# RWKV chunks of 64 tokens instead of 32, two heads on the partitions and four beside, 64x64 inverses joined from blocks of 32

## The chip, the cores and the metric

One core of a Trainium2 chip runs the whole program. The metric is the device time of one execution in microseconds; the median of several is compared. Five engines work side by side: TensorE (PE, with its weight loads PEld), VectorE (DVE), ScalarE (ACT), GpSimd (POOL) and SyncE (SP), which issues most transfers.

## The reference

A trunk of two mixing layers, each followed by a squared-ReLU MLP, on 512 tokens of width 1024 in float32. Layer 0 splits its input projection between a Griffin recurrence (512 columns wide) and RWKV-7 time mixing (8 heads of 64); layer 1 has gated DeltaNet and mLSTM. The change is in RWKV. After the token shift, decays and norms, what it computes is this recurrence over the tokens:

```
def step(S, inp):
    rt, wt, kt, vt, kkt, at = inp
    sk = jnp.einsum('bhvk,bhk->bhv', S, kkt)
    S = (S * wt[:, :, None, :] - sk[..., None] * (kkt * at)[:, :, None, :]
         + vt[..., None] * kt[:, :, None, :])
    return S, jnp.einsum('bhvk,bhk->bhv', S, rt)
```

y is then normed per head, gets a bonus (r, k, r_k) times v, is gated by g, joined with the Griffin output and projected back.

## The kernel before

Large matrices are split into a high and a low fp32r part and multiplied in three matmuls (wh h, wh l, wl h) of 128x128 by 512 columns. The projections are streamed: raw weights come by DMA, ScalarE or VectorE casts the high part (wh), VectorE or GpSimd makes the low part (wl). The names `hT` with `wh`, `wl` are the input projection; `wh`, `wl` with `yah`, `yal` the Griffin half of the output projection, with `ybh`, `ybl` its RWKV half, which comes last.

RWKV is computed in chunks of 32 tokens, 16 chunks, with products inside a chunk as matrices, so that a chunk's state change is a few small fp32 matmuls (an fp32 matmul shows as two MATMUL records and two weight loads). For two halves of the tokens (hf 0 and 1, eight chunks each) the steps are:

- `product_stream` (L882): alpha and rho (`va`) against kappa and beta (`kb`), 256 matmuls of 64x32 by 64 columns, masked on VectorE into `cm`, four heads one over the other on the partitions, two beside.
- `inverse_stream` (L962): the lower triangular 32x32 blocks go through memory into one block per lane (partition), `lanes` (L936) inverts them there with 62 dependent VectorE operations (`xtmp`, `xt` on `q`), and the inverses come back through memory as `xb`. `lanes` runs once per half.
- `turn_stream` (L905): `va` and `kb` transposed against the identity into `tm`, 512 matmuls.
- `ahead_stream` (L983): `wt`, `bv`, `u0` from `tm`, `cm` and `xb`, all that does not hang on the state.
- `scan_stream` (L1033): 16 steps; in each one group of 8 matmuls with the state `S`, an add on VectorE to `us`, groups with `us`, and an add on VectorE into the next `S`. The heads' norm and gate (`heads_stream`, L1090) hang behind.

Beside this runs Griffin: convolution (`xc`), gates (`r`, `i`, `th`), a scan on VectorE, and `gel` times the result split into `yah` and `yal`. All engines' instructions are issued through one helper (L73), so every row of the profile has line L73 and is told apart by its names.

The order of the instructions on each engine is decided while the kernel is built: `layer0` (L1255) spawns the streams, the one spawned first has the highest priority, and a planner keeps a clock per engine with the prices of `cost` (L173); a stream that needs a tile (`need`) or an event waits in the plan, and the lowest priority, the main stream with the large projections, fills the gaps. A psum bank is taken with `take` and returned with `give`; there are 8.

## Time and profile before

| | |
|---|---|
| time, median of 3 runs | 1405.82 us (1405.06 to 1406.92) |
| profiled execution | 1407.12 us, span 1405.3 us |
| TensorE busy | 1334.4 us (95% of the span) |
| VectorE busy | 768.4 us (55%) |
| ScalarE busy | 472.2 us (34%) |
| GpSimd busy | 184.2 us (13%) |
| mean granted TensorE clock | 0.975 |

TensorE is busy nearly always, but a busy stretch is not one of full use: many small matmuls, a lower granted clock and short stops lie in it. Layer 0 takes the stretch from the start to some 340 us, and RWKV's small matmuls lie between 95 and 310 us. An "issue" releaser is time in which an engine waited for nothing that the profile shows. The granted clock is a share of full speed.

### The profile page before, as it was taken

How to read it: one execution, taken by the hardware profiler on the slowest of the kernel's cores; microseconds unless marked ns; L12 is line 12 of the kernel's file. 1: busy time of each engine (PE TensorE's matmuls, PEld its weight loads, DVE VectorE, ACT ScalarE, POOL GpSimd, SP SyncE). 2: the span in 40 equal slices, each digit the busy share in tenths (PEclk: the TensorE clock that was granted, in tenths of full speed). 3: DMA queues.
4: the chain of work that ended last, by engine and by line, in shares of the span. 5: the costliest groups of instructions: out<-in, count | busy, mean ns of one | idle time of the engine just before them, and what ended most of it. 6: DMA issues, size and time to landing. Idle time of an engine off the chain costs nothing.

```text
span 1405.3 us, 23951 instructions
## 1 busy us (share of the span) xinstructions
PE 1334.4 (95%) x10036; PEld 1079.7 (77%) x10036; DVE 768.4 (55%) x1444; ACT 472.2 (34%) x818; POOL 184.2 (13%) x172
## 2 busy tenths in 40 slices
PE   6888999899999999999999999999789999999998
PEld 6666777668888888888896777878578888888886
DVE  5885956456434435344568748854744354453444
ACT  5522523324322323223453434431333232232222
POOL 2352221231000000000013412213300000000000
PEclk9999989999999999999999999999989999999999
DMA  6122200322233233232312231110322322322331
GB/s 228 61 82 86 69 19 24 100 87 76 88 96 99 90 93 102 90 91 98 112 54 83 76 97 61 49 57 16 120 76 63 102 90 90 105 91 90 97 99 60
DMA packets 58594, 118.35 MB, mean 84 GB/s; under 512 B 17398, under 2 KB 17654, under 8 KB 58486
## 3 DMA queue, kind: packets, MB, share of 16 engines
q1 hardware_dynamic: 57190, 114.71, 25.8%
q10 hardware_dynamic: 1296, 2.11, 0.5%
q8 instruction: 79, 1.29, 0.4%
q14 instruction: 29, 0.24, 0.1%
HBM read 113.13 MB, written 3.67 MB: 83 GB/s over the span
## 4 chain that ended last, share of the span: by engine, by line
PE 83%; DVE 7%; issue 3%; ACT 3%; DMA 3%; POOL 1%; SPq 0%; POOLq 0%; DVEq 0%
PE ps_a L73 61%; PE ps_g L73 23%; DMA q<-d1g 1%; DMA q<-d 1%; DVE xn L73 1%; DVE wl L73 1%; DVE x L73 1%; DVE ktok L73 1%; DMA gb<-in_g_norm_dram 0%; ACT junk L73 0%; DVE cv L73 0%; DVE gr L73 0%; DVE z L73 0%; ACT k L73 0%; ACT wh L73 0%
## 5 line engine op out<-in xcount | busy, mean ns | idle before, releaser
L73 DVE TENSOR_TENSOR wl<-raw,wh 128x512 fp32r<-128x512 f32 x325 | 232.0, 720 | 257.8 <-ACT wh L73 249.1
L73 PE MATMUL ps_a<-hT,wh 128*128 128x512 f32 (+1 forms) x1088 | 315.5, 375 | 0.0
L73 ACT CAST wh<-raw 128x512 fp32r<-128x512 f32 x283 | 172.4, 619 | 361.5 <-PE ps_a L73 317.9
L73 PEld LDWEIGHTS ps_a<-hT,wh 128*128 128x128 f32 x1088 | 197.3, 188 | 41.0
L73 PE MATMUL ps_g<-hT,wh 128*128 128x512 f32 x656 | 218.7, 413 | 7.7 <-DVE xt L73 3.7
L73 PE MATMUL ps_a<-hT,wl 128*128 128x512 f32 (+1 forms) x544 | 203.8, 375 | 0.0
L73 PEld LDWEIGHTS ps_g<-hT,wh 128*128 128x128 f32 x656 | 127.0, 195 | 43.2 <-issue 11.1
L73 PE MATMUL ps_a<-wh,acth 128*128 128x512 f32 x384 | 151.5, 395 | 0.0
L73 PE MATMUL ps_a<-wl,acth 128*128 128x512 f32 x384 | 151.5, 395 | 0.0
L73 PE MATMUL ps_a<-wh,actl 128*128 128x512 f32 x384 | 151.3, 394 | 0.0
L73 PE MATMUL ps_g<-hT,wl 128*128 128x512 f32 x328 | 134.8, 411 | 0.0
L73 POOL TENSOR_TENSOR wl<-raw,wh 128x512 fp32r<-128x512 f32 x43 | 57.6, 1346 | 580.9 <-ACT wh L73 557.3
L73 PEld LDWEIGHTS ps_a<-hT,wl 128*128 128x128 f32 x544 | 102.1, 188 | 20.4
L73 PEld LDWEIGHTS ps_a<-wh,actl 128*128 128x128 f32 x384 | 72.1, 188 | 17.1
L73 PEld LDWEIGHTS ps_a<-wh,acth 128*128 128x128 f32 x384 | 72.2, 188 | 16.8
L73 PEld LDWEIGHTS ps_a<-wl,acth 128*128 128x128 f32 x384 | 72.1, 188 | 16.8
L73 DVE CAST wh<-raw 128x512 fp32r<-128x512 f32 x85 | 37.1, 436 | 86.9 <-PE ps_a L73 82.0
L73 ACT ACTIVATE relu<-ps_a 128x512 f32<-128x512 f32 x60 | 35.9, 599 | 141.6 <-PE ps_a L73 141.6
L73 PEld LDWEIGHTS ps_g<-hT,wl 128*128 128x128 f32 x328 | 64.0, 195 | 17.4 <-issue 2.1
L73 PE MATMUL ps_g<-hT,w 128*128 128x256 f32 x384 | 51.2, 290 | 0.4 <-DVE hT L73 0.4
L73 PE MATMUL ps_g<-wh,acth 128*128 128x512 f32 x128 | 50.5, 395 | 0.0
L73 PE MATMUL ps_g<-wl,acth 128*128 128x512 f32 x128 | 50.5, 395 | 0.0
(395 smaller groups left out, 1820.4 us busy)
## 6 DMA issues: line engine op xcount, KB each, us to landing
...
```

The costliest lines, as they stand in the source:

```text
L73: return fn(*args, **kw)
```

## The change

The chunks are 64 tokens, 8 of them. Two heads lie on the partitions (64 rows each) and four beside each other, so all small tiles are 64x64 and `HEADS` names only the two diagonal quarters of the array. `product_stream` makes 128 matmuls with 128 columns, and splits each bank on VectorE in two masked operations, into `ab` (for m = 1; `bk` for m = 0) and `mm`; its last quarter waits for the first half's inverse. The lanes still invert 32x32 blocks, now the two diagonal blocks of each 64x64 one; the off-diagonal block (`A`, masked with `join`) is then brought in by three rounds of matmuls: `xb` transposed into `xs`, `A` times `xs` into `xg`, and `xg` times `xb`, added to `xb`. `ahead_stream` has one helper for wt, bv and u0, the scan has one bank and one addition per step, `v` is shifted by one VectorE operation, and the planner's price of a small matmul is higher. TensorE's small fp32 matmuls are 2024 before and 1184 after.

```diff
-        return self.sp.tile([P, 3, 4, 16, 32], dt, tag="wide", bufs=1, name=f"{name}{self.n}")
+        return self.sp.tile([P, 3, 4, 8, 64], dt, tag="wide", bufs=1, name=f"{name}{self.n}")
...
-            return max(n / 600, 0.107) + 0.002 if size(a) == P else 0.045
+            return max(n / 600, 0.107) + 0.002 if P in (size(a), a.shape[0]) else max(n / 1200, 0.053)
...
-        self.rmask = self.cst[:, 128:192]
-        o = 192
+        o = 128
         for name, n in (("inc64", P), ("suf64", P), ("inc128", P), ("suf128", P), ("ones", P), ("pair", 2), ("lt64", 64), ("le64", 64), ("join", 64)):
             setattr(self, name, self.cst[:, o:o + n])
+            if name == "lt64":
+                self.ltle = self.cst[:, o:o + P]
...
-        return ap.rearrange("p (c s) -> p c s", s=32)
+        return ap.rearrange("p (c s) -> p c s", s=64)
...
-            nc, c3 = self.nc, self.c3
-            v = self.va[:, 0, p]
-            nc.scalar.activation(out=v, in_=c3(ps), func=AF.Identity, scale=self.omu[:, 8 + p:9 + p])
-            mu = self.col("mu", 8 + p)
-            nc.vector.scalar_tensor_tensor(out=v[:, :, 1:32], in0=c3(ps)[:, :, 0:31], scalar=mu, in1=v[:, :, 1:32], op0=ALU.mult, op1=ALU.add)
-            nc.vector.scalar_tensor_tensor(out=v[:, 1:16, 0:1], in0=c3(ps)[:, 0:15, 31:32], scalar=mu, in1=v[:, 1:16, 0:1], op0=ALU.mult, op1=ALU.add)
+            self.shift_mix(ps, 8 + p, self.va[:, 0, p].rearrange("p c s -> p (c s)"))
...
-    HEADS = [(i, b, e, slice(64 * b, 64 * b + 64), slice(64 * i + 32 * b, 64 * i + 32 * b + 32), slice(64 * e, 64 * e + 64))
-             for e in range(2) for i in range(2) for b in range(2)]
+    HEADS = [(q, slice(64 * b, 64 * b + 64)) for q in range(4) for b in range(2)]
...
-        for hf in range(2):
-            for m in (1, 0):
-                for j in (2 * hf, 2 * hf + 1):
-                    ps = yield from self.take()
-                    v = ps.rearrange("p (c e t) -> p c e t", e=2, t=64)
-                    for c in range(4):
-                        for i, b, e, f, r, _ in self.HEADS:
-                            nc.tensor.matmul(v[r, c, e, :], lhsT=self.kb[f, m, 2 * i + e, 4 * j + c, :], rhs=self.va[f, 1:3, 2 * i + e, 4 * j + c, :],
-                                             start=True, stop=True)
-                        yield
-                    o = self.slot(shape=(P, 8, 64), name="cm")
-                    nc.vector.tensor_tensor(out=o, in0=ps.rearrange("p (c t) -> p c t", t=64), in1=self.rmask[:, None, :].broadcast_to([P, 8, 64]), op=ALU.mult)
-                    self.give(ps)
-                    self.cm[m][j] = o
-                self.set(f"cm{m}{hf}")
+        for m, hf in ((1, 0), (1, 1), (0, 0), (0, 1)):
+            if m == 0 and hf:
+                yield "xb0"
+            ab, mm = (self.bk, self.mv) if m == 0 else (self.ab, self.mu)
+            ab[hf] = self.slot(shape=(P, 4, 4, 64), tag="q", name="ab")
+            for j in (2 * hf, 2 * hf + 1):
+                mm[j] = self.slot(shape=(P, 2, 4, 64), name="mm")
+            for c in range(4 * hf, 4 * hf + 4):
+                ps = yield from self.take()
+                v = ps.rearrange("p (q t) -> p q t", q=4)
+                for q, r in self.HEADS:
+                    nc.tensor.matmul(v[r, q], lhsT=self.kb[r, m, q, c, :], rhs=self.va[r, 1:3, q, c, :], start=True, stop=True)
+                for k, (o, mask) in enumerate(((ab[hf][:, c % 4], self.lt64), (mm[c // 2][:, c % 2], self.le64))):
+                    nc.vector.tensor_tensor(out=o, in0=v[:, :, 64 * k:64 * k + 64], in1=mask[:, None, :].broadcast_to([P, 4, 64]), op=ALU.mult)
+                self.give(ps)
+                yield
+            self.set(f"cm{m}{hf}")
...
-            for k, src in enumerate((self.va[:, 0], self.va[:, 1], self.kb[:, 0], self.kb[:, 1])):
+                self.tt(w, w, self.pc[:, :, cs, None].broadcast_to([P, 4, 4, 64]), ALU.mult)
+            for k, src in ((1, self.va[:, 1]), (0, self.va[:, 0]), (2, self.kb[:, 0]), (3, self.kb[:, 1])):
                 for j in (2 * hf, 2 * hf + 1):
                     yield self.need(src)
                     ps = yield from self.take()
...
+                    v = ps.rearrange("p (c q x) -> p c q x", c=2, q=4)
+                    for c in range(2):
+                        for q, r in self.HEADS:
+                            nc.tensor.matmul(v[r, c, q], lhsT=src[r, q, 2 * j + c, :], rhs=self.ident[r, r], start=True, stop=True)
+                    o = self.slot(shape=(P, 2, 4, 64), name="tm")
+                    self.cpy(o.rearrange("p c q x -> p (c q x)"), ps)
                     self.give(ps)
...
-                if k in (1, 3):
-                    self.set(f"tm{k}{hf}")
+                self.set(f"tm{k}{hf}")
...
-        d1 = self.dp.tile([4, 8, 2, 32, 32], F32, name=f"d1_{hf}")
-        for j in range(2):
-            cm = self.cm[1][2 * hf + j]
-            yield self.need(cm)
-            for p in range(4):
-                nc.sync.dma_start(out=d1[p, 4 * j:4 * j + 4].rearrange("c e s t -> s (c e) t"), in_=cm[32 * p:32 * p + 32, :, 0:32])
+        d1 = self.dp.tile([4, 16, 32, 32], F32, name=f"d1_{hf}")
+        A = self.ab[hf].rearrange("p c q t -> p (c q) t")
+        yield self.need(A)
+        for g in range(4):
+            o = g % 2 * 32
+            nc.sync.dma_start(out=d1[g].rearrange("l s t -> s l t"), in_=A[32 * g:32 * g + 32, :, o:o + 32])
         at = self.slot(shape=(P, 32, 32), tag="q")
-        xt = yield from self.lanes(d1.rearrange("p c e s t -> (p c e) s t"), at)
+        lanes = self.lanes(d1.rearrange("g l s t -> (g l) s t"), at)
+        yield next(lanes)
+        self.tt(A, A, self.join[:, None, :].broadcast_to([P, 16, 64]), ALU.mult)
+        xt = yield from lanes
         d2 = yield from self.leave(xt, f"d2_{hf}")
-        xb = self.slot(shape=(P, 16, 32), name="xb")
-        yield self.need(d2)
-        for p in range(4):
+        xb = self.slot(shape=(P, 16, 64), tag="q", name="xb")
+        nc.gpsimd.memset(xb, 0.0)
+        yield self.need(d2, xb)
+        for g in range(4):
...
-                nc.sync.dma_start(out=xb[32 * p + q:32 * p + 32:2], in_=d2[q, 16 * p:16 * p + 16].rearrange("l m t -> m l t"))
-        self.xb[hf] = xb
+                nc.sync.dma_start(out=xb[32 * g + q:32 * g + 32:2, :, o:o + 32], in_=d2[q, 16 * g:16 * g + 16].rearrange("l m t -> m l t"))
...
+        for i in range(2):
+            ps = yield from self.take()
+            for l in range(8):
+                for r in rows:
+                    nc.tensor.matmul(ps[r, l * 64:l * 64 + 64], lhsT=xb[r, 8 * i + l, :], rhs=self.ident[r, r], start=True, stop=True)
+            xs.append(self.slot(shape=(P, 8, 64), name="xs"))
...
+            for l in range(8):
+                for r in rows:
+                    nc.tensor.matmul(ps[r, l * 64:l * 64 + 64], lhsT=A[r, 8 * i + l, :], rhs=xs[i][r, l, :], start=True, stop=True)
+            gs.append(self.slot(shape=(P, 8, 64), name="xg"))
...
+            for l in range(8):
+                for r in rows:
+                    nc.tensor.matmul(ps[r, l * 64:l * 64 + 64], lhsT=gs[i][r, l, :], rhs=xb[r, 8 * i + l, :], start=True, stop=True)
+            x = xb[:, 8 * i:8 * i + 8]
+            nc.vector.tensor_tensor(out=x, in0=ps.rearrange("p (l t) -> p l t", l=8), in1=x, op=ALU.add)
+            self.give(ps)
+            yield
+        self.xb[hf] = xb.rearrange("p (c q) t -> p c q t", q=4)
         self.set(f"xb{hf}")
...
+        def products(a, b, name):
+            ps = yield from self.take()
+            v = ps.rearrange("p (c q x) -> p c q x", c=2, q=4)
+            for c in range(2):
+                for q, r in self.HEADS:
+                    nc.tensor.matmul(v[r, c, q], lhsT=a[r, c, q, :], rhs=b[r, c, q, :], start=True, stop=True)
+            o = self.slot(shape=(P, 2, 4, 64), name=name)
+            self.cpy(o.rearrange("p c q x -> p (c q x)"), ps)
+            self.give(ps)
+            yield
+            return o
...
+                yield self.need(xb, self.tm[1][j], self.tm[0][j])
+                self.wt[j] = yield from products(self.tm[1][j], xb[:, c], "wt")
+                bv = yield from products(self.bk[hf][:, c], self.tm[0][j], "bv")
                 yield self.need(bv)
-                ps = yield from self.take()
...
+                self.u0[j] = yield from products(xb[:, c], bv, "u0")
...
-        us = self.slot(shape=(P, 4, P), name="us")
-        self.in_parts(us, P)
-        for c in range(16):
-            j, c4 = c // 4, c % 4
+        us = self.slot(shape=(P, 2, 4, 64), name="us")
+        self.in_parts(us, 256)
+        quarters = lambda ap: ap.rearrange("p (q x) -> p q x", x=64)
+        for c in range(8):
+            j, h = c // 2, c % 2
             S0, S1 = S[:, c % 2], S[:, (c + 1) % 2]
...
-                for i, b, e, f, r, x in self.HEADS:
-                    nc.tensor.matmul(ps[r, x], lhsT=wt[i][f, e, c % 8, :], rhs=S0[f, i, e, :], start=True, stop=True)
-                u = us[:, c4]
-                nc.vector.tensor_tensor(out=u, in0=ps[:, 0:P], in1=u0[:, c4, :], op=ALU.add)
+                v = quarters(ps[:, 0:256])
+                for q, r in self.HEADS:
+                    nc.tensor.matmul(v[r, q], lhsT=wt[r, h, q, :], rhs=S0[r, q, :], start=True, stop=True)
...
+            if c < 7:
                 if c:
                     tt = self.slot(shape=(P, 4, 64), tag="tt", bufs=2)
-                    self.tt(tt, S0.rearrange("q i e v -> q (i e) v"), self.pc[:, :, c:c + 1].broadcast_to([P, 4, 64]), ALU.mult)
-                ps = yield from self.take_all("aa")
-                for i, b, e, f, r, x in self.HEADS:
-                    nc.tensor.matmul(ps[i][f, x], lhsT=kt[r, c4, x], rhs=vt[r, c4, x], start=(e == 0), stop=False)
-            for i, b, e, f, r, x in self.HEADS:
-                nc.tensor.matmul(vy[r, c4, x], lhsT=cm[0][r, 2 * c4 + e, 32:64], rhs=vt[r, c4, x], start=(c4 == 0 and e == 0), stop=False)
+                    self.tt(tt, S0, self.pc[:, :, c:c + 1].broadcast_to([P, 4, 64]), ALU.mult)
+                ps = yield from self.take()
+                v = quarters(ps[:, 0:256])
+                for q, r in self.HEADS:
+                    nc.tensor.matmul(v[r, q], lhsT=kt[r, h, q, :], rhs=vt[r, h, q, :], start=(q == 0), stop=False)
+            for q, r in self.HEADS:
+                nc.tensor.matmul(vy[r, h, q], lhsT=mv[r, h, q, :], rhs=vt[r, h, q, :], start=(h == 0 and q == 0), stop=False)
...
-            if c < 15:
-                for i, b, e, f, r, x in self.HEADS:
-                    nc.tensor.matmul(ps[i][f, x], lhsT=bt[r, c4, x], rhs=u[r, x], start=False, stop=(e == 1))
-                for i in range(2):
-                    v = ps[i][:, 0:P].rearrange("p (e v) -> p e v", v=64)
-                    if c:
-                        nc.vector.tensor_tensor(out=S1[:, i], in0=v, in1=tt[:, 2 * i:2 * i + 2], op=ALU.add)
-                    else:
-                        self.cpy(S1[:, i], v)
-                self.give(*ps)
-            for i, b, e, f, r, x in self.HEADS:
-                nc.tensor.matmul(vy[r, c4, x], lhsT=cm[1][r, 2 * c4 + e, 32:64], rhs=u[r, x], start=False, stop=(c4 == 3 and e == 1))
-            if c4 == 3:
+            if c < 7:
+                for q, r in self.HEADS:
+                    nc.tensor.matmul(v[r, q], lhsT=bt[r, h, q, :], rhs=u[r, q, :], start=False, stop=(q == 3))
+                if c:
+                    nc.vector.tensor_tensor(out=S1, in0=v, in1=tt, op=ALU.add)
+                else:
+                    self.cpy(S1, v)
+                self.give(ps)
+            for q, r in self.HEADS:
+                nc.tensor.matmul(vy[r, h, q], lhsT=mu[r, h, q, :], rhs=u[r, q, :], start=False, stop=(h == 1 and q == 3))
+            if h:
                 self.spawn(self.heads_stream(j, psy))
```

Two places of the order. TensorE at the first use of the half-0 inverse (`xb`), before: the last rows are input projection, then follow the ahead stage, transposes of the second half and the first scan step.

```order
L73 MATMUL ps_g_1891<-hT_108,wl_1848 128x512
L73 MATMUL ps_g_1936<-hT_106,wh_1865 128x512
L73 MATMUL ps_g_1936<-hT_107,wh_1865 128x512
L73 MATMUL ps_a_1944<-xb_1786,tm_1465 64x32 x16
L73 MATMUL ps_a_1944<-xb_1786,tm_1505 64x32 x16
L73 MATMUL ps_a_1979<-xb_1786,tm_1465 64x32 x16
L73 MATMUL ps_a_1979<-xb_1786,tm_1505 64x32 x16
L73 MATMUL ps_a_2016<-tm_1385,cm_975 32x64 x32
L73 MATMUL ps_a_2062<-idn,va_352 32x64 x32
L73 MATMUL ps_a_2097<-bv_2049,xb_1786 32x64 x32
L73 MATMUL ps_a_2133<-tm_1424,cm_1010 32x64 x32
L73 MATMUL ps_a_2166<-tm_1385,tm_1546 64x64 x2
```

After, at the first use of `xb` (here as `idn,xb`, the first round of the join):

```order
L73 MATMUL ps_g_1780<-hT_108,wh_1698 128x512
L73 MATMUL ps_g_1780<-hT_109,wh_1698 128x512
L73 MATMUL ps_g_1780<-hT_108,wl_1699 128x512
L73 MATMUL ps_a_1885<-idn,xb_1732 64x64 x16
L73 MATMUL ps_a_1904<-idn,xb_1732 64x64 x16
L73 MATMUL ps_g_1923<-wh_1746,yah_1849 128x512
L73 MATMUL ps_g_1923<-wl_1747,yah_1849 128x512
L73 MATMUL ps_g_1923<-wh_1746,yal_1850 128x512
L73 MATMUL ps_a_1936<-xs_1902,ab_857 64x64 x16
L73 MATMUL ps_g_1924<-wh_1746,yah_1849 128x512
L73 MATMUL ps_g_1924<-wl_1747,yah_1849 128x512
L73 MATMUL ps_g_1924<-wh_1746,yal_1850 128x512
```

Before, 111 input-projection matmuls stand between the first half's transposes and this place, and 70 behind the first half's scan; after, all 191 that are left stand ahead of it, and the Griffin half of the output projection is what TensorE has left beside RWKV.

VectorE around the Griffin output `yah`, before (the wl rows are weights of the projections, the th and i rows Griffin's gates):

```order
L73 CAST wh_3146<-raw_1996 128x512
L73 TENSOR_TENSOR wl_3147<-raw_1996,wh_3146 128x512
L73 MEMSET th_2991 128x1
L73 TENSOR_TENSOR i_2989<-i_2989,th_2991 128x512
L73 SCALAR_TENSOR_TENSOR th_2991<-xc_1840,i_2989 128x512
L73 MEMSET th_3056 128x1
L73 TENSOR_TENSOR i_3054<-i_3054,th_3056 128x512
L73 SCALAR_TENSOR_TENSOR th_3056<-xc_1886,i_3054 128x512
L73 TENSOR_TENSOR gel_1934<-gel_1934,th_1768 128x512
L73 CAST yah_3176<-gel_1934 128x512
L73 TENSOR_TENSOR yal_3177<-gel_1934,yah_3176 128x512
```

After, the last operations of the second lane chain (`xtmp`, `xt`), then Griffin's gates and `yah`:

```order
L73 TENSOR_TENSOR xt_1015<-xt_1015,xtmp_1016 128x15x2
L73 TENSOR_TENSOR xtmp_1016<-xt_1015,q_1014 128x16
L73 TENSOR_TENSOR xt_1015<-xt_1015,xtmp_1016 128x16
L73 MEMSET th_1682 128x1
L73 TENSOR_TENSOR i_1676<-i_1676,th_1682 128x512
L73 SCALAR_TENSOR_TENSOR th_1682<-xc_1528,i_1676 128x512
L73 MEMSET th_1721 128x1
L73 TENSOR_TENSOR i_1714<-i_1714,th_1721 128x512
L73 SCALAR_TENSOR_TENSOR th_1721<-xc_1577,i_1714 128x512
L73 CAST yah_1849<-gel_1627 128x512
L73 TENSOR_TENSOR yal_1850<-gel_1627,yah_1849 128x512
```

Both lane chains now lie ahead of `yah`, and the evictions of the first half's ahead stage and scan, which lay ahead of it before, lie behind it.

## Rows read from the trace of the kernel before

**Rows 1.** The page: instruction queue (packets, MB, share); chain of waits by engine.

```profile
q8 instruction: 79, 1.29, 0.4%
...
PE 83%; DVE 7%; issue 3%; ACT 3%; DMA 3%; POOL 1%; SPq 0%; POOLq 0%; DVEq 0%
```

**Rows 2.** What TensorE waited for, 95 to 318 us: total, times, longest.

```profile
PE ps_a L73 <- issue: 14.2, 12, 2.3
PE ps_g L73 <- DVE yah L73: 4.9, 1, 4.9
```

**Rows 3.** By stage: length, busy PE, PEld, DVE, ACT, POOL, granted clock, DMA, GB/s.

```profile
113.10:150.20 37.10, 33.67 (x607) 26.82 (x606) 24.52 (x70) 13.36 (x22) 7.65 (x5) 0.94 0.27 85
150.20:179.70 29.50, 29.50 (x128) 22.26 (x119) 27.66 (x67) 16.66 (x23) 11.93 (x9) 1.00 0.26 73
179.70:228.40 48.70, 43.62 (x1706) 37.30 (x1705) 21.21 (x63) 9.20 (x18) 4.91 (x8) 0.82 0.03 10
228.40:250.50 22.10, 22.08 (x153) 16.44 (x150) 18.20 (x39) 13.36 (x19) 2.31 (x2) 1.00 0.18 47
...
257.50:317.60 60.10, 56.91 (x1358) 43.18 (x1358) 28.08 (x62) 13.48 (x23) 17.58 (x17) 0.94 0.27 85
```

**Rows 4.** Timeline of TensorE, products and transposes: start, length, records, idle before.

```profile
97.18 3.42 PE L73 MATMUL ps_a<-va,kb 64*32 64x64 f32 x226 [1.68 <-POOL va L73]
...
106.02 1.99 PE L73 MATMUL ps_a<-va,kb 64*32 64x64 f32 x128 [2.01 <-issue]
...
144.94 5.37 PE L73 MATMUL ps_a<-idn,kb 64*32 64x64 f32 x248 [2.33 <-issue]
```

**Rows 5.** Timeline of TensorE: scan groups, wt (xb,tm) and u0 (bv,xb) matmuls.

```profile
192.39 0.43 PE L73 MATMUL ps_a<-S,wt 64*32 64x64 f32 x16
192.75 0.46 PE L73 MATMUL ps_a<-tm,tm 32*64 32x64 f32 x16
...
263.88 2.79 PE L73 MATMUL ps_a<-xb,tm 32*64 32x32 f32 x96
...
269.38 1.09 PE L73 MATMUL ps_a<-bv,xb 32*32 32x64 f32 x64
```

**Rows 6.** Timeline of TensorE in layer 1, 64x64 tiles.

```profile
933.60 1.15 PE L73 MATMUL ps_a<-xtr,ds 64*64 64x64 f32 x32
934.68 0.50 PE L73 MATMUL ps_g<-wh,ydh 128*128 128x512 f32 x1
...
951.05 1.08 PE L73 MATMUL ps_a<-u,dq 64*64 64x128 f32 x8
```

**Rows 7.** Stretches with small tiles: columns as in rows 3.

```profile
181.80:185.20 3.40, 3.40 (x108) 3.34 (x106) 3.10 (x10) 1.83 (x4) 0.00 (x0) 0.63 0.04 11
263.40:300.80 37.40, 36.23 (x1194) 26.87 (x1192) 13.57 (x39) 6.28 (x11) 5.00 (x7) 1.00 0.08 26
915.00:1000.00 85.00, 81.68 (x612) 66.33 (x611) 45.78 (x86) 20.93 (x36) 20.49 (x19) 1.00 0.15 46
```

**Rows 8.** VectorE by operation, 129 to 242 us: busy, mean ns of one, idle before.

```profile
L73 DVE TENSOR_TENSOR xtmp<-xt,q 128x126 f32<-128x126 f32 (+22 forms) x62 | 19.9, 330 | 1.2 <-DMA q<-d 0.2
L73 DVE TENSOR_TENSOR xt<-xt,xtmp 128x126 f32<-128x126 f32 (+22 forms) x62 | 16.7, 280 | 1.1
L73 DVE TENSOR_TENSOR wl<-raw,wh 128x512 fp32r<-128x512 f32 x11 | 11.0, 1001 | 0.6 <-ACT wh L73 0.2
L73 DVE SCALAR_TENSOR_TENSOR xc<-ps_g,par,xc 128x511 f32<-128x511 f32 (+2 forms) x12 | 9.0, 746 | 1.0 <-ACT xc L73 0.8
...
L73 DVE TENSOR_TENSOR_SCAN th<-xc,i 128x512 f32<-128x512 f32 x2 | 2.4, 1218 | 0.0
...
L73 DVE TENSOR_TENSOR i<-i,th 128x512 f32<-128x512 f32 x2 | 1.4, 694 | 0.1
```

**Rows 9.** SyncE's issues of the first half's inverse, out and back.

```profile
162.43 0.33 SPq L73 DMA_DIRECT2D d<-xt  x1
...
165.10 5.24 SPq L73 DMA_DIRECT2D xb<-d  x8
```

124 lines of the change are left out of this document (47 added, 77 removed).

## The prediction

> **What bounds the kernel now.** I read the page's chain of waits first: 83% of it is TensorE [rows 1], so the stretch counts as long as TensorE's order takes to run through it. The order of the instructions shows which stretch that is: from the first small products (95.1 us of the trace) to the first projection of the RWKV outputs (317.6 us), 222.5 us in all; what comes behind has the same instructions in the same order in both kernels, so the end moves by what this stretch gains or loses. The view of what TensorE waits for gives two large names there: "issue", 14.2 us in twelve gaps, and the Griffin output yah, 4.9 us [rows 2]. The table by stage gives the rest: full-size work runs without a hole (29.5 us busy of 29.5, 128 matmul records, 0.23 us each), while the RWKV work on the first half of the tokens, from 179.7 to 228.4, is granted a clock of 0.82 and VectorE is far from full in it, 21.2 us of 48.7 [rows 3].
>
> **The twelve gaps.** In the timeline a gap stands before each batch of 128 matmul records of small tiles (1.99 us long, after 2.01 us of nothing), and one of 2.33 us stands before 248 records that then take 5.37 us [rows 4]. Each record has a weight load beside it. In the stretches of large matmuls there is no such gap [rows 3]. So I read them as TensorE running out of instructions: 128 records pass in 2.0 us and the next 128 are there some 3.2 us (1.99 and the mean gap, 14.2/12) to 4.0 us (1.99 + 2.01) after the former. The page has a queue for instructions, 79 packets and 1.29 MB, 16.3 KB each [rows 1].
>
> **The change, term by term, TensorE in this stretch.** An fp32 matmul is two records; I price one matmul.
>
> *Issue gaps.* The small matmuls fall from 2024 to 1184, and each lasts longer (below, 59 ns against about 30). 128 records then take 64 x 0.059 = 3.8 us, about what the next need (3.2 to 4.0). I leave 2 us of the 14.2: -12.
>
> *Array work.* Before: a 64x32 tile product costs 1.99/64 = 0.031 us [rows 4]; a scan group of eight starts 0.36 us after the former; the wt matmuls (32x64 tiles) cost 2.79/48 = 0.058 and the u0 ones 1.09/32 = 0.034, as I take bv too [rows 5]. After: all tiles are 64x64, two beside each other where four were. The trace has that form in layer 1: 16 matmuls take 934.68 - 933.60 = 1.08 us, switch to the next shape included [rows 6]; without a switch I take 0.059. For 128 columns I take twice that, 0.118; the row for 64x128 on one half alone (1.08/4 = 0.27) is its upper bound and half of it, 0.135, what two halves beside each other would give [rows 6]. Then:
> products 256 x 0.031 = 7.9 become 128 x 0.118 = 15.1, +7.2;
> transposes 512 x 0.031 = 15.9 become 256 x 0.059 = 15.1, -0.8;
> the three stages of the join are new, 192 x 0.059 = +11.3;
> wt, bv and u0, 128 x (0.058 + 0.034 + 0.034) = 16.1, become 192 x 0.059 = 11.3, -4.8;
> the scan, 93 groups of eight x 0.36 = 33.5, becomes 44 groups x 8 x 0.059 = 20.8, or 44 x 0.54 = 23.8 if each group costs half of a batch of 1.08; -12.7 to -9.7;
> heads halve in number at twice the price, 0.
> Sum 0.2 to 3.2; I take +2. So the array does not get less to do; bounds -2 and +7 (the upper one with 0.135 for products and 0.067, which is 1.08/16, for all others).
>
> *Clock.* Lost time before is length times what lacks of 1.0: 37.1 x 0.06 + 48.7 x 0.18 + 60.1 x 0.06 = 14.6 us [rows 3]. The low stretches follow idle TensorE (the gap of 2.33 us ahead of the 5.37 us batch [rows 4], the wait for yah [rows 2]), and once they set in with no gap ahead, at 181.8 under 32x32 tiles (0.63) [rows 7]. Small tiles between full-size ones were at 1.00 from 263.4 to 300.8, and so was layer 1 with its 64x64 tiles [rows 7]. After, most gaps are gone, but a long wait (below) is new: about 3 us behind it and 6 for dips in the scan's waits: 9, so -6. Bounds -12 to +2.
>
> *VectorE and the new wait.* The new order runs all 191 remaining input-projection matmuls ahead of the first use of an inverse; before, the scan of the first half stood between them. The transposes of the first half end near 138 instead of 150: 97.2, where the products get going [rows 4], + 96 x 0.118 + 82 x 0.23 of the projection + 4 fp32 ones at 0.46 + 128 x 0.059 + about 1 of waiting (10 projection matmuls, the last products and four gaps no longer stand ahead). The projection is through at 138 + 191 x 0.23 + 8 fp32 gate matmuls of two records, 0.46 = 186, or 188 with some slow clock. Then it needs xb (joined inverse) and yah, yal. VectorE has, in its order between the transposes' evictions (about 135) and yah: 113 lane operations at (0.330 + 0.280)/2 = 34.5; 11 wl at 1.00 = 11.0; 12 xc at 0.75 = 9.0; 4 scans at 1.22 = 4.9; 16 others of the full width at no more than 0.69 = 11.0 [rows 8]: 70.4 us at most, or 67.0 with wl at the undisturbed 0.69. These means hold what VectorE loses while GpSimd works, as the mask and the kb products will again make it. So yah stands near 202.5 (135 + 67) and the first yal some 2 us behind it, at 204.5, if VectorE hardly pauses. The inverse of the first half comes earlier: lane 0 ends after 126 of the 160 rows, near 187, then out and back through memory as before (162.43 until the eight xb transfers are issued, 165.10 + 5.24 = 170.34 [rows 9]): 8 us and their landing, near 197. TensorE stands from 188 to 204.5 but for 2.5 us of the join's transposes: 14 us of wait in place of 4.9: +9. This is the change's largest cost and it is hidden by nothing, since all projections have been used up. Bounds: +4 (yal at 199.5) to +24 (the first rival).
>
> *Waits between scan steps.* 16 steps become 8. The chain of a step (wt matmuls, add on VectorE, us matmuls, add) has 0.47 us groups to lie behind instead of 0.36: from no change to -4, taken -3. The eight instead of sixteen transfers into memory, the mask and the memsets on GpSimd, v's one VectorE operation instead of two lie beside TensorE's work.
>
> Sum: -12 + 2 - 6 + 9 - 3 = **-10 us**. The profiled span 1405.3 becomes 1395.3; the run it belongs to took 1407.1, the median is 1405.8, so the median goes to **1396**.
>
> A rule of the Trainium skill speaks against the first term. "Runtime: NRT & Kernel Launch", Instruction fetch mechanics, says that the sequencer fetches the next block of 256 instructions while it runs the current one, and that crossing a block is mostly hidden. The trace agrees with the block (128 records and as many weight loads between gaps) and not with "hidden" (2.01 and 2.33 us in the two rows, 1.2 on the mean). By that rule the gaps would be of other origin; its mechanism is the third rival.
>
> **Rivals.**
> (1) Slower: VectorE pauses. The sum has it working through from 135 to 202.5. In 228.4 to 250.5, with lanes and Griffin work alike, it was busy 18.2 of 22.1 us, 82%; from 150.2 to 179.7 it was 94% [rows 3]. The lane chains and Griffin's gates wait on ScalarE and on each other. At 80%, 67 us take 84, yal stands near 220, 15 later than in my sum: +5, **1411**. It decides from yal at 217 (+2.8). For my sum: two lane chains now lie beside each other over most of it, as in the 94% stretch. 0.22.
> (2) Clock. From 213 to about 283 TensorE has hardly any full-size work between 64x64 tiles; if this runs at 0.82 as 179.7 to 228.4 did, 70 x 0.18 = 12.6 us are lost instead of 6, and with dips in the transposes some 2 more: about -1.5, **1404**. Against it: the 1.00 rows in [rows 7]. 0.10.
> (3) The gaps do not follow the count of instructions, and stay: +12, so +2, **1408**. For it is that no row tells a gap's cause; against it that all twelve lie in dense small tiles. 0.08.
> (4) More gain: yal at 199.5 (-5), no dips in the scan (-6): **1385**. 0.12.
>
> **How the numbers follow.** My forecast, 1390 to 1402, has 0.48. This kernel's measurement can tell about 0.2%, 2.8 us, from no change. Faster: 0.48 + 0.12 + a little of (2) = 0.61. Same: most of (2) and half of (3), 0.13. Slower: (1) and half of (3), 0.26. The range that holds 8 in 10 leaves out the far half of (4) and the far third of (1): 1383 to 1412. The gaining cases' own range is 1383 to 1402.
>
> **What would show it.** Right, if the view of waits between 95 us and the first RWKV output projection has "issue" at 1 to 4 us; TensorE ends the input projection at 186 to 190 and then waits 10 to 20 us for xb, yah and yal together; 16 matmuls of 64x64 tiles start 0.9 to 1.1 us apart; that output projection starts near 307.6. Wrong, if issue gaps remain at 8 or more, if yal comes after 217, if the granted clock behind it stays near 0.8, or if anything behind the output projection differs by more than 2 us.

## The result

The changed kernel takes 1370.65 us (1367.48 to 1374.06, four runs) against 1406.37 us for the kernel before (1405.06 to 1407.23): the ratio is 0.9747, with a 95% interval of 0.9717 to 0.9777. That is 35.7 us faster. The forecast was 10 us faster, 1396, with a range of 1383 to 1412; the sign was right, the size was not, and the time lies below the range.

The profiled execution of the changed kernel took 1372.95 us. From its page, the span, TensorE's row of the busy times, the instruction queue and the chain of waits:

```profile
span 1371.2 us, 20609 instructions
...
PE 1309.5 (95%) x8372; PEld 1078.5 (79%) x8372; DVE 773.1 (56%) x1435; ACT 476.1 (35%) x823; POOL 193.3 (14%) x172
...
q8 instruction: 66, 1.08, 0.3%
...
PE 81%; DVE 10%; ACT 3%; issue 2%; DMA 2%; POOL 1%; SPq 0%; DVEq 0%; POOLq 0%; ACTq 0%
```

TensorE has 8372 matmul records instead of 10036, the instruction queue 66 packets instead of the 79 of [rows 1], and the chain is TensorE's to 81% instead of 83%.

Where the 34.1 us of the span went is read from the starts of six landmarks in TensorE's timeline: the first small product (`va,kb`), the first RWKV output projection (`wh,ybh`), the first matmul of the first MLP's second half (`acth`), layer 1's first gate transpose (`idn,gf`), the second MLP's `acth`, and the last matmul. The lengths between them, in us:

| piece | before | after | difference |
|---|---|---|---|
| start to first product | 95.1 | 98.1 | +3.0 |
| RWKV stretch: first product to RWKV output projection | 222.6 | 203.1 | -19.5 |
| to first `acth` | 72.5 | 72.1 | -0.4 |
| to layer 1 (first MLP) | 331.9 | 329.6 | -2.3 |
| layer 1, to second `acth` | 363.9 | 350.5 | -13.4 |
| second MLP, to the last matmul | 312.4 | 310.8 | -1.6 |

So the gain has two large parts: 19.5 us in the stretch that the prediction was about, for which it had 10, and 13.4 us in layer 1, for which it had nothing. Nor had it anything for the 3.9 us of the two MLPs or the 3.0 us lost at the start.

**The RWKV stretch.** What TensorE waited for in it (columns as in [rows 2]):

```profile
PE ps_a L73 <- DMA xb<-d: 6.9, 2, 4.7
PE ps_a L73 <- issue: 4.0, 1, 4.0
PE ps_g L73 <- DVE yah L73: 3.1, 1, 3.1
...
PE ps_g L73 <- DVE yal L73: 0.4, 1, 0.4
...
PE ps_a L73 <- DVE us L73: 0.2, 1, 0.2
```

Against [rows 2], 14.2 us of issue in twelve gaps have become one of 4.0 us, and the wait for the Griffin output (yah 4.9) has become 6.9 for the inverse, 3.1 for yah and 0.4 for yal. The one "issue" that is left is none of the old kind. It stands between two large pieces of work, ahead of Griffin's gate matmuls:

```profile
155.74 3.00 PE L73 MATMUL ps_a<-xc,wlru 128*128 128x512 f32 x4 [3.97 <-issue]
```

and VectorE's timeline shows what they read being made until 153.32 + 2.31 = 155.63:

```profile
153.32 2.31 DVE L73 SCALAR_TENSOR_TENSOR xc<-ps_g,par,xc 128x511 f32<-128x511 f32 x3
```

I read it as a wait for xc, whose last operation ends 0.1 us ahead of it, and which the profile could not name. The gaps of [rows 4] are all gone.

By stage (columns as in [rows 3]): products and transposes; the rest of the input projection; the wait; the first matmuls behind it; all the rest:

```profile
98.10:140.80 42.70, 41.38 (x540) 34.89 (x539) 25.87 (x52) 12.76 (x21) 12.55 (x12) 1.00 0.34 95
140.80:197.60 56.80, 52.79 (x207) 39.37 (x207) 51.16 (x135) 29.38 (x40) 15.93 (x13) 0.97 0.13 47
197.60:212.90 15.30, 5.00 (x67) 4.04 (x67) 14.62 (x30) 7.05 (x12) 8.34 (x5) 0.72 0.64 190
212.90:218.40 5.50, 5.50 (x45) 4.07 (x47) 2.75 (x5) 1.57 (x4) 0.00 (x0) 0.54 0.41 140
218.40:301.20 82.80, 82.43 (x1944) 75.29 (x1941) 45.12 (x87) 25.61 (x45) 18.71 (x17) 1.00 0.14 43
```

VectorE is busy 51.2 of 56.8 us beside the projection and 14.6 of 15.3 in the wait: I read it as the bound there. Behind it, for 82.8 us with 1944 matmul records, TensorE is busy 82.4 at a clock of 1.00, the upper of its two levels (2.4 GHz), where [rows 3] had 0.82 for the comparable 48.7 us; the 0.72 and 0.54 are stretches partly at the lower level (1.2 GHz), in and right behind the stops between 197.6 and 211.3. The wait itself, in TensorE's timeline:

```profile
202.28 0.44 PE L73 MATMUL ps_a<-idn,xb 64*64 64x64 f32 x2 [4.72 <-DMA xb<-d]
204.88 3.32 PE L73 MATMUL ps_a<-idn,xb 64*64 64x64 f32 x62 [2.17 <-DMA xb<-d]
211.27 0.77 PE L73 MATMUL ps_g<-wh,yah 128*128 128x512 f32 x1 [3.06 <-DVE yah L73]
...
212.86 0.80 PE L73 MATMUL ps_g<-wh,yal 128*128 128x512 f32 x1 [0.40 <-DVE yal L73]
```

SyncE's issues of the first half's inverse show why `xb` was late too:

```profile
192.36 0.33 SPq L73 DMA_DIRECT2D d<-xt  x1
197.54 0.33 SPq L73 DMA_DIRECT2D raw<-in_w_out_dram  x1
197.98 5.24 SPq L73 DMA_DIRECT2D xb<-d  x8
```

From the way out to the first `xb` transfer 5.6 us pass, where [rows 9] had 2.7: a weight transfer stood ahead of `xb` in SyncE's queue and left at 197.54, 0.02 us after VectorE ended a wl (196.83 + 0.69). I read it as VectorE's queue holding back `xb` as well.

Products (180 records, 90 fp32 matmuls, 0.112 us each) and transposes (0.061 each) run without a gap:

```profile
100.31 10.04 PE L73 MATMUL ps_a<-va,kb 64*64 64x128 f32 x180 [1.32 <-POOL va L73]
...
136.90 3.90 PE L73 MATMUL ps_a<-idn,kb 64*64 64x64 f32 x128
```

And a scan step of 64 tokens, six groups of eight; the `idn,xb` batch belongs to the second half's join:

```profile
233.74 0.63 PE L73 MATMUL ps_a<-S,wt 64*64 64x64 f32 x16
234.20 0.63 PE L73 MATMUL ps_a<-tm,tm 64*64 64x64 f32 x16
...
236.54 1.11 PE L73 MATMUL ps_a<-idn,xb 64*64 64x64 f32 x32
237.47 0.64 PE L73 MATMUL ps_a<-S,wt 64*64 64x64 f32 x16
```

Groups start 0.46 us after each other; a step is six of them, 2.8 us (233.74 to 236.54). Before, a step of half as many tokens took about as long or longer: its six groups at 0.36 to 0.39 are 2.2 us and other batches and gaps lay between ([rows 5] shows the groups).

An account of the whole stretch, made by giving the time from each row's start to the next row's, less the idle time ahead of that, to the kind of matmul: small fp32 matmuls of RWKV 87.8 us before, 80.9 after (products 8.2 to 14.3, transposes 20.1 to 15.2, join 0 to 14.3, the rest 59.5 to 37.1); large ones (projections, gates, g) 110.7 to 106.1; idle 24.1 to 16.0.

**Layer 1.** The last part of layer 1, from the first output projection with the split weights (`w,ych`) to the second MLP's input. Before, the stage row and the largest waits:

```profile
996.90:1039.50 42.60, 32.90 (x129) 23.73 (x130) 27.02 (x55) 15.17 (x35) 13.59 (x11) 0.88 0.21 72
```

```profile
PE ps_g L73 <- ACT ych L73: 4.0, 3, 1.8
PE ps_a L73 <- POOL o L73: 2.0, 1, 2.0
PE ps_a L73 <- DVE xn L73: 2.0, 3, 1.1
PE ps_g L73 <- DVE w L73: 1.9, 1, 1.9
```

After:

```profile
977.40:1005.60 28.20, 26.41 (x125) 20.77 (x126) 19.98 (x39) 10.25 (x25) 8.18 (x7) 1.00 0.30 103
```

```profile
PE ps_g L73 <- DVE x L73: 2.0, 1, 2.0
PE ps_a L73 <- DVE xn L73: 1.2, 2, 0.7
```

42.6 us have become 28.2: TensorE's idle time in it falls from 9.7 (42.60 - 32.90) to 1.8 us (28.20 - 26.41; the wait for x lies just ahead of this piece), and the clock rises from 0.88 to 1.00. The two kernels' order differs there; before, the last outputs that the projection needs (o, ych) come while it already waits for them, after, they have come earlier. Nothing in layer 1's code is changed by the diff, but `cost` is: layer 1 has small fp32 matmuls too (64x64 ones in gated DeltaNet), and the planner orders them by that price.

**The MLPs.** TensorE's order in both MLPs is the same in every profile of this study, and the clock is 1.00. What differs is the pace of the full-size matmuls that read `hT`. A block of 192 of them, before; the same block after; and a block of the second MLP after (the counts take in one or two neighbours that overlap the ends):

```profile
434.60:479.40 44.80, 44.80 (x193) 35.91 (x193) 23.02 (x40) 14.20 (x23) 0.00 (x0) 1.00 0.31 94
```

```profile
417.90:461.90 44.00, 44.00 (x194) 36.09 (x193) 23.04 (x40) 14.21 (x23) 0.00 (x0) 1.00 0.28 96
1098.10:1142.90 44.80, 44.80 (x194) 36.28 (x193) 23.04 (x40) 14.20 (x23) 0.00 (x0) 1.00 0.27 94
```

That is 0.233 us per matmul or 0.229. The 576 of an MLP take 134.4 us before and 131.9 and 132.7 after, which is the whole of the 2.3 and 1.6 us in the table; matmuls that read `acth` lie 0.232 apart in both kernels. The RWKV stretch has 273 such matmuls, so some 1.2 us of its 19.5 may be this pace (an estimate: 273 x 0.0044).

### The profile page after: what moved, and what is told of

It reads as the page before. It is cut to its first block, busy times and chain, and to the rows that moved or that the text cites. A ratio compares the mean times of both kernels' runs of the same rounds, so it can differ in the third digit from the quotient of the medians.

```text
span 1371.2 us, 20609 instructions
## 1 busy us (share of the span) xinstructions
PE 1309.5 (95%) x8372; PEld 1078.5 (79%) x8372; DVE 773.1 (56%) x1435; ACT 476.1 (35%) x823; POOL 193.3 (14%) x172
## 4 chain that ended last, share of the span: by engine, by line
PE 81%; DVE 10%; ACT 3%; issue 2%; DMA 2%; POOL 1%; SPq 0%; DVEq 0%; POOLq 0%; ACTq 0%
PE ps_a L73 61%; PE ps_g L73 20%; DVE wl L73 1%; DMA q<-d1g 1%; DVE xn L73 1%; DVE xtmp L73 1%; DVE xt L73 1%; DVE th L73 1%; DVE sft L73 1%; DVE x L73 1%; DVE ktok L73 0%; DMA gb<-in_g_norm_dram 0%; POOL w L73 0%; ACT junk L73 0%; DVE cv L73 0%
## 5 line engine op out<-in xcount | busy, mean ns | idle before, releaser
L73 PEld LDWEIGHTS ps_g<-hT,wh 128*128 128x128 f32 x656 | 125.4, 193 | 42.1 <-issue 13.6
L73 PE MATMUL ps_g<-hT,wl 128*128 128x512 f32 x328 | 130.6, 398 | 0.0
L73 POOL TENSOR_TENSOR wl<-raw,wh 128x512 fp32r<-128x512 f32 x39 | 52.2, 1349 | 553.9 <-ACT wh L73 553.9
L73 PEld LDWEIGHTS ps_a<-wl,acth 128*128 128x128 f32 x384 | 72.1, 188 | 17.0
L73 PEld LDWEIGHTS ps_a<-wh,acth 128*128 128x128 f32 x384 | 72.1, 188 | 16.7
L73 PE MATMUL ps_g<-wh,actl 128*128 128x512 f32 x128 | 50.5, 394 | 0.0
```

The costliest lines, as they stand in the source:

```text
L73: return fn(*args, **kw)
```

## The experiments

The comparison of each is with the kernel before on the same chip. The pieces are those of the table above.

### The price of a small matmul in the planner, and nothing else

```diff
-            return max(n / 600, 0.107) + 0.002 if size(a) == P else 0.045
+            return max(n / 600, 0.107) + 0.002 if P in (size(a), a.shape[0]) else max(n / 1200, 0.053)
```

Four kernels: the kernel before with this line; the changed kernel without it; and each with the other price from the start of layer 1 on only (a flag that layer1 sets and `cost` reads).

> The kernel before, chunks of 32 and all its tiles, with the changed kernel's price of small fp32 matmuls in the planner and nothing else. The trace of the changed kernel has 19.5 us of its 34 us inside the stretch from the first products to the first RWKV output projection, and some 15 us in layer 1, where the order of the instructions turns out to differ. Theory A (the price alone reorders layer 1, and that is worth the 15 us): the whole takes about 1391, layer 1 from its first gate transposes (idn,gf) to the last MLP's first matmul about 303 us instead of 317; layer 0 within 5 us of before. Theory B (layer 1 gains because layer 0 ends elsewhere, or by chance of a run): about 1406, layer 1 at 317.

> The changed kernel with the old price of small matmuls in the planner. Theory A: layer 1 falls back to the order of before and to about 317 us, the whole takes about 1386; layer 0 keeps its 19.5 us, give or take what the other price does to the order there. Theory B: about 1371, layer 1 at 303.

> The kernel before with the new price from the start of layer 1 on only: layer 0 is instruction for instruction that of before. Theory A: 1391, with the stretch up to the first RWKV output projection as before (317.6 us). Theory B: 1406.

> The changed kernel with the old price from the start of layer 1 on: layer 0 is instruction for instruction that of the changed kernel. Theory A: about 1386, the first RWKV output projection at 301, layer 1 at about 317 us. Theory B: 1371, layer 1 at 303.

The kernel before beside these four took 1411.41 us, and their ratios go by that.

| kernel | median, us | ratio to before, 95% interval | RWKV stretch | layer 1 |
|---|---|---|---|---|
| before (profile shown) | 1406.37 | | 222.6 | 363.9 |
| before, new price | 1393.46 | 0.9871 (0.9841 to 0.9900) | 223.8 | 355.0 |
| before, new price in layer 1 | 1399.96 | 0.9919 (0.9899 to 0.9940) | 221.9 | 357.4 |
| changed (profile shown) | 1370.65 | 0.9747 (0.9717 to 0.9777) | 203.1 | 350.5 |
| changed, old price in layer 1 | 1385.09 | 0.9807 (0.9786 to 0.9828) | 202.6 | 365.5 |
| changed, old price | 1382.33 | 0.9799 (0.9777 to 0.9821) | 208.4 | 355.0 |

With layer 0 untouched, the price in layer 1 alone takes 0.8% off the whole, and 6.5 us off layer 1 in the profile; with the changed layer 0, giving the old price back to layer 1 alone makes layer 1 15.0 us longer. So layer 1 does move by the order that the price makes, and theory B alone falls. Theory A's 303 and 317 were read with other landmarks, but its shift of some 15 us holds in the changed kernel (15.0) and is only half there in the kernel before (6.5).

The last row shows that theory B holds for the rest. With the old price throughout, TensorE's order in layer 1 is that of the kernel before but for one batch of transposes, and layer 1 takes 355.0 us instead of 363.9: 8.9 us come with the changed layer 0 and next to no other order. With the new price, the order in the changed kernel is that of the kernel before with the new price in layer 1, again but for one batch of transposes, and layer 1 takes 350.5 us instead of 357.4: 6.9 us, again with layer 0. So of the 13.4 us, the order that the price makes brings 4.5 to 6.5, and 6.9 to 8.9 come with the changed layer 0 in front of nearly the same order. From 363.9 to 355.0 TensorE's idle time falls from 23.7 to some 21 us, its mean clock rises from 0.97 to 0.98, and the pace of the `hT` matmuls is another; what brings these with layer 0 was not tried and stays open. Nor is the last part of layer 1, shown above, all gain: with the new price in layer 1 of the kernel before it shrinks by as much, 13.3 us (42.5 to 29.2), while layer 1 shrinks by 6.5, since the parts around it grow.

The size of this has a scatter. The nine profiles with the new price in layer 1 have 346.1 to 357.4 us there, the four with the old one 355.0 to 365.5, and four profiles with one and the same order 352.8 to 357.4 (the two kernels before with the new price and two edits of the changed kernel below, Griffin first and the second half's lanes behind the first's). What is shown is that replanning alone, layer 0 unchanged instruction for instruction, moves layer 1 by up to 15 us with no change to its work. In layer 0 the new price is worth 5 us to the changed kernel (208.4 to 203.1, or 202.6) and nothing to the kernel before (223.8 against 222.6).

### Again, and three edits of the changed kernel

> The changed kernel once more, to stand beside the others of this group: about 0.975 of before, the first RWKV output projection at about 301 us.

It took 1371.54 us (ratio 0.9757, 0.9739 to 0.9775); its pieces are within 1 us of the first profile (RWKV stretch 203.7, layer 1 349.6). So pieces of two profiles of this kernel can be set against each other to about 1 us.

**Narrow matmuls**, to bring the gaps back:

```diff
-                        for q, r in self.HEADS:
-                            nc.tensor.matmul(v[r, c, q], lhsT=src[r, q, 2 * j + c, :], rhs=self.ident[r, r], start=True, stop=True)
+                        for u in range(2):
+                            for q, r in self.HEADS:
+                                cols = slice(r.start + 32 * u, r.start + 32 * u + 32)
+                                nc.tensor.matmul(v[r, c, q, 32 * u:32 * u + 32], lhsT=src[r, q, 2 * j + c, :], rhs=self.ident[r, cols], start=True, stop=True)
...
-                for q, r in self.HEADS:
-                    nc.tensor.matmul(v[r, q], lhsT=self.kb[r, m, q, c, :], rhs=self.va[r, 1:3, q, c, :], start=True, stop=True)
+                for u in range(2):
+                    for q, r in self.HEADS:
+                        nc.tensor.matmul(v[r, q, 64 * u:64 * u + 64], lhsT=self.kb[r, m, q, c, :], rhs=self.va[r, 1 + u, q, c, :], start=True, stop=True)
```

> The changed kernel with the products issued as two matmuls of 64 columns and the transposes as two of 32 columns: the same work for the array, the same 64x64 tiles, and 384 small matmuls more (768 records, as many weight loads). Theory A (the twelve gaps of before come from the rate at which TensorE uses up instructions): gaps named issue, one per 128 records, come back inside the products and transposes, 4 to 8 us in all, with a lower granted clock behind some, and the stretch up to the first RWKV output projection grows from 203 to 208 to 213 us. Rival (the gaps belong to the 64x32 and 32x32 tile shapes, four beside each other): no gaps, stretch 203 to 205. If a matmul of 32 columns costs more than half of one of 64, it shows in the pace inside the batches, apart from the gaps.

1375.3 us (ratio 0.9786, 0.9756 to 0.9817), the stretch 212.3. Its products and its transposes against kb:

```profile
99.97 10.60 PE L73 MATMUL ps_a<-va,kb 64*64 64x64 f32 x356 [1.18 <-POOL va L73]
...
140.78 7.63 PE L73 MATMUL ps_a<-idn,kb 64*64 64x32 f32 x256
```

No gap came back (the one wait named issue in the stretch, 3.8 us, is again the one ahead of Griffin's gates), but the premise failed too: 256 records of 32 columns take 7.63 us, 0.060 per matmul, as long as one of 64 columns; 64 columns on 64x64 tiles take 10.60/178 = 0.060. TensorE did not use up its instructions any faster, so this run says nothing on the gaps. The stretch grew because twice as many transposes cost twice the time (15.2 to 30.0 us in the account, while the waits fell by 5.7), so it ended within theory A's 208 to 213 for another reason.

**Griffin first**: `lru_stream` ahead of `inverse_stream(1)` in the spawn of layer0.

```diff
-                   self.lora_stream(), self.pair_stream(3), self.product_stream(), self.inverse_stream(1), self.turn_stream(), self.lru_stream())
+                   self.lora_stream(), self.pair_stream(3), self.product_stream(), self.lru_stream(), self.inverse_stream(1), self.turn_stream())
```

> The changed kernel with Griffin's stream ahead of the second half's inverse in the planner's priorities, so that VectorE makes yah and yal ahead of the rest of the second lane chain. In the changed kernel TensorE stood from 197.6 to 212.9 us for xb, yah and yal. Theory A (VectorE's queue sets that wait): yah comes earlier, by some 5 us, and TensorE's wait between the input projection and the Griffin half falls from 13 to 8 us or less; the whole 3 to 6 us faster than the changed kernel, about 1366. Rival (xb, through memory, sets it anyway, or the second inverse is late in exchange): within 2 us of the changed kernel or slower.

1378.25 us (ratio 0.9811, 0.9796 to 0.9826), 7 us slower than the changed kernel beside it. The wait did not go away:

```profile
202.34 3.65 PE L73 MATMUL ps_a<-idn,xb 64*64 64x64 f32 x62 [2.36 <-DMA xb<-d]
209.60 0.77 PE L73 MATMUL ps_g<-wh,yah 128*128 128x512 f32 x1 [3.62 <-DVE yah L73]
```

yah comes at 209.6 instead of 211.3, and TensorE still stands for xb and yah; the order that came out put the Griffin half of the projection ahead of the scan, so that RWKV's output projection starts at 292.2 but the first `acth` only 85.0 us on instead of 72. The priority of one stream is not the lever: VectorE has nearly the same work ahead of yah in either order (118 of the 124 lane operations instead of all).

**Tile shapes in the scan.** Two of six groups per step on 64x32 tiles:

```diff
-                    nc.tensor.matmul(v[r, q], lhsT=wt[r, h, q, :], rhs=S0[r, q, :], start=True, stop=True)
+                    for w in range(2):
+                        f = slice(r.start + 32 * w, r.start + 32 * w + 32)
+                        nc.tensor.matmul(v[f, q], lhsT=wt[r, h, q, 32 * w:32 * w + 32], rhs=S0[r, q, :], start=True, stop=True)
...
-                nc.tensor.matmul(vy[r, h, q], lhsT=mv[r, h, q, :], rhs=vt[r, h, q, :], start=(h == 0 and q == 0), stop=False)
+                for w in range(2):
+                    f = slice(r.start + 32 * w, r.start + 32 * w + 32)
+                    nc.tensor.matmul(vy[f, h, q], lhsT=mv[r, h, q, 32 * w:32 * w + 32], rhs=vt[r, h, q, :], start=(h == 0 and q == 0), stop=False)
```

> The changed kernel with two of the six groups of a scan step (wt times S, and mv times v) issued on 64x32 tiles, sixteen matmuls four beside each other instead of eight two beside each other: the same array time (16 x 0.029 against 8 x 0.058), 120 small matmuls more. Theory A (before, each change of the tile shape between groups cost TensorE 0.13 us, and the scan of before gained its price from that): each of these groups is followed and led by a change; start to start it takes 0.55 to 0.6 us instead of 0.466 and a step 3.1 to 3.4 us instead of 2.8; the stretch grows by 3 to 5 us. Rival (a change of shape is free and the scan of before was slow by clock and waits alone): a step at 2.8 us, the stretch within 1 us.

1369.27 us (ratio 0.9746, 0.9728 to 0.9764), not told apart from the changed kernel beside it (0.9757). The scan step in its timeline:

```profile
232.99 0.65 PE L73 MATMUL ps_a<-S,wt 64*32 64x64 f32 x32
233.57 0.68 PE L73 MATMUL ps_a<-tm,tm 64*64 64x64 f32 x16
234.18 0.65 PE L73 MATMUL ps_a<-tm,mm 64*32 64x64 f32 x32
234.76 0.68 PE L73 MATMUL ps_a<-S,va 64*64 64x64 f32 x16
235.28 0.63 PE L73 MATMUL ps_a<-us,tm 64*64 64x64 f32 x16
...
236.21 1.10 PE L73 MATMUL ps_a<-idn,xb 64*64 64x64 f32 x32
237.25 0.65 PE L73 MATMUL ps_a<-S,wt 64*32 64x64 f32 x32
```

Groups at or just behind a change start the next one 0.52 to 0.61 us on, and the two at the end of the step, on one shape, 0.46; the step takes 236.21 - 232.99 = 3.22 us instead of 2.80. From one S,wt to the next, with the same idn,xb batch between, it is 237.25 - 232.99 = 4.26 us instead of 237.47 - 233.74 = 3.73: 0.53 for four changes, 0.13 each. Theory A holds in its price. In the account the scan's groups grew by 2.2 us (21.6 to 23.8) and the stretch by 1.6, less than the 3 to 5 expected; layer 1 came out 4.4 us shorter (346.1), replanned once more, and hid it in the whole.

### The gaps, in the kernel before

```diff
+        idw = self.small((P, 4, 64), "li").rearrange("p a b -> p (a b)")
+        nc.gpsimd.memset(idw, 0.0)
+        for q in range(2):
+            f = slice(64 * q, 64 * q + 64)
+            nc.gpsimd.tensor_copy(out=idw[f, 64:128], in_=self.ident[f, f])
...
-                            nc.tensor.matmul(v[r, c, x], lhsT=src[f, 2 * i + e, 4 * j + c, :], rhs=self.ident[f, f], start=True, stop=True)
+                            nc.tensor.matmul(v[r, c], lhsT=src[f, 2 * i + e, 4 * j + c, :], rhs=idw[f, 64 - 64 * e:192 - 64 * e], start=(e == 0), stop=(e == 1))
```

> The kernel before with its 512 transposes against a 64x128 piece [identity, zero] or [zero, identity], two adding up in one place: the same 64x32 tiles, the same count and order of instructions, but 128 columns streamed, so that one lasts about 0.056 us instead of 0.030 and 128 records about 3.6 us instead of 2.0. Theory A (gaps come from using up instructions faster than they arrive): the gap of 2.33 us ahead of the batch against kb and those inside the second half's transposes go; issue falls from 14.2 to some 6 to 9 us (the products' three, 5.7 us, and some in the scan stay); the stretch up to the first RWKV output projection grows by 13 for the columns less 5 to 8. Rival (the tile shape makes the gaps): 12 to 14 us of issue stay, the stretch grows by 13 or more.

1407.54 us, ratio 1.0010 (0.9986 to 1.0035). What TensorE waited for, and a batch of products and the transposes against kb in the timeline:

```profile
PE ps_a L73 <- issue: 7.6, 9, 2.0
```

```profile
103.80 1.99 PE L73 MATMUL ps_a<-va,kb 64*32 64x64 f32 x128 [2.01 <-issue]
...
144.69 7.25 PE L73 MATMUL ps_a<-li,kb 64*32 64x128 f32 x254
```

Products, untouched, still stop 2.01 us ahead of 128 records. The transposes against kb, same 64x32 tiles and same number of instructions as in [rows 4] but 0.057 us each, run through 254 records with no gap. Issue falls to 7.6, as theory A had it, from 14.2 in the profile of before and 17.7 and 16.2 in the two other profiles with chunks of 32 (new price; new price in layer 1), and the stretch grows by 7.3 us (222.6 to 229.9) though 512 transposes last 0.027 longer each, 13.8 us: the rest is paid by the gaps. So the tile shape is not what makes them; the gaps go with the rate at which TensorE runs through its records.

The DMA records of the traces show what a gap waits for. The packets of the instruction queue (q8 of [rows 1], 16 KB each) come one by one, and in the four profiles with chunks of 32 all 51 issue gaps of the stretch end 1.0 to 1.7 us after the end of such a packet. In the kernel before, packets end at 100.7, 104.7 and 108.6 us, and TensorE goes on at 102.0, 106.0 and 110.3. The second of them, in the view of the DMA queues from 103.1 to 104.8:

```profile
q8 instruction: 1, 0.02, 5.4%
```

In the changed kernel the one wait that is named issue ends 15.1 us after the last such packet, so it is of another kind.

### The join, and the order of the lanes

The join left out (the lines from `rows = [...]` to the addition into `xb`), so that the inverse lacks its off-diagonal block:

> The changed kernel without the join: the three matmul rounds and the addition that bring the off-diagonal block into the inverse are left out, so what the join costs is seen. By the account of the changed kernel's trace the join holds TensorE for 14.3 us in the stretch. Theory A (it is paid in full, on TensorE's path): the stretch shortens by 10 to 15 us. Rival (half of it lies in the wait for yah, which would be waited for anyway): by 5 to 8 us.

1360.14 us, ratio 0.9661 (0.9628 to 0.9693); the stretch is 192.0 instead of 203.1, 11.1 us shorter, of the 14.3 that the account gives the join. It is paid nearly in full.

The second half's lanes behind the first's:

```diff
+        if hf:
+            yield next(lanes)
+            yield "lane0"
         xt = yield from lanes
+        self.set(f"lane{hf}")
```

> The changed kernel with the second half's lane operations held back until the first half's are done, instead of interleaved with them. Theory A (TensorE's 13 to 15 us of waits at 197.6 to 212.9 come from VectorE's queue, where both lane chains lie ahead of xb and yah): xb comes 8 to 15 us earlier, TensorE does the join and the scan between the input projection's matmuls, waits there fall to under 6 us, and the stretch shortens by 5 to 10 us; some 1363 in all. Rival (VectorE has the same work ahead of yah or only moves the wait to the second half's inverse): the stretch within 3 us of 203.

1372.71 us, ratio 0.9741 (0.9714 to 0.9767), against 0.9747 and 0.9757 for the two measurements of the changed kernel. The largest waits of the stretch:

```profile
PE ps_a L73 <- DVE yn L73: 5.8, 2, 5.2
PE ps_a L73 <- ACT xs L73: 4.7, 1, 4.7
```

The join's first round now stands ahead of the projection's end and yah is used only from 243.8, but 4.7 us of waiting for the join's copy and 5.8 for the heads' norm have come in its place. The stretch is 199.0 (4 us shorter, under the 5 to 10 expected) and 3.3 of the 4 are lost again before the first `acth` (75.4 instead of 72.1). No version here that keeps the join beats the changed kernel beyond its interval.

## Why the prediction was off

**"What comes behind has the same instructions in the same order", so it takes the same time: wrong, and the costliest step.** For the two MLPs the order was right. For layer 1 it was not: I compared the order too coarsely there. The diff's line in `cost` reprices layer 1's small matmuls, and the order differs. And the same order did not take the same time. Where I had nothing, the runs show 13.4 us less in layer 1 (4.5 to 6.5 by the order that the price makes, 6.9 to 8.9 with the changed layer 0 in front of nearly the same order), 3.9 less in the two MLPs (the pace of the `hT` matmuls, at the same order) and 3.0 more at the start, where TensorE's listed waits for xn and k rise from 13.6 to 19.1 us. The prediction's own sign, a difference of more than 2 us behind the output projection, tells it wrong. Had the order listings been compared row by row to the end, layer 1 would have been a term with an unknown sign of 10 us or more, and a wider range. None of this is work that larger chunks save; only a part of it is shown to be replanning.

**Issue gaps, -12: right.** They went entirely (-14.2), and the reading of them holds: the wide transposes have slower records, the same shape and no gap, and every gap of before ends just behind an instruction packet. The rule of the Trainium skill that I weighed ("Runtime: NRT & Kernel Launch", Instruction fetch mechanics: crossing a block is mostly hidden) holds in this trace where records are slow and does not where 128 of them pass in 2.0 us.

**Array +2 and clock -6, together -4: the mis-sized term of the stretch.** The account gives -11.5 for both: 6.9 for small matmuls and 4.6 for large ones. What the array does after was priced well: the products at 0.112 (0.118 taken), everything else at 0.058 to 0.061 (0.059 taken), no cost between groups; a scan at a clock of 0.82 (rival 2) did not come. How the account divides scatters, though. The kernel before with the new price in layer 1 only has layer 0 instruction for instruction as before; against its stretch (221.9) the two terms together fall by 6.6 (193.6 to 187.0) and the waits by 12.3 (28.3 to 16.0). The whole stretch in the kernel before, in that repeat, and after:

```profile
95.10:317.60 222.50, 198.12 (x4458) 156.35 (x4458) 134.07 (x314) 71.35 (x113) 52.43 (x50) 0.92 0.23 66
```

```profile
94.80:316.70 221.90, 193.62 (x4458) 151.78 (x4458) 133.98 (x314) 71.60 (x113) 52.20 (x50) 0.95 0.23 66
```

```profile
98.10:301.20 203.10, 187.10 (x2795) 157.66 (x2795) 139.51 (x307) 76.37 (x120) 55.52 (x47) 0.96 0.23 68
```

Length times what lacks of 1.00 is some 18, 11 and 8 us, so the clock brought -10 against the one profile and -3 against the other, on either side of my -6. What is left for the array is some -2 to -4 (an estimate; the pace of the `hT` matmuls is 1.2 of it) where I had +2. Its upper bound was added up wrongly as well: with 0.135 and 0.067 the items come to over +10 and not +7. I would have put the better clock down to the gaps, but the repeat has them in full (16.2 us of issue) at nearly the clock of after: no run here shows that the gaps cause the low clock.

**The new wait, +9: right in size by luck.** At this place TensorE waits 10.4 us against 5.3 of yah and yal before, +5.1; only with the 4.0 us for xc, which my sum did not have, is it +9.1. And yal comes at 212.9 and not at 204.5. The stretch began 3 us later, the projection ended at 197.6 and not 188 (xc, and the low clock behind it), `xb` was there at 204.88 and not near 197, and VectorE needed from 138 to 211, 73 us, for what I had at 67 and rival (1) at 84. The stretch as a whole did not become slower, because the rest behind it took 88.3 us (212.9 to 301.2) where my sum had 103.

**Waits between scan steps, -3: there was nothing to gain.** The waits listed for the stretch before name no scan tile (us, S): besides issue, yah and yal they are x with 1.9 us and va with 2.8. After, us has 0.2. The 3 us came mostly from x (none after) and va (1.3 after). The scan gained otherwise: there is no change of tile shape between its groups any more, which costs 0.13 each when it is put back in.

**Rivals.** (1) did not come: VectorE took 73 us and yal came ahead of 217. (2) did not occur. (3) is refuted: the gaps went, and each of them had followed an instruction packet. (4), more gain, had the sign of the miss but only 12 in 100 of chance and none of its place.
